# Gate matrices in a queue of their own, with two stages, their one-hots multiplied on GpSimd

## The chip, the cores and the metric

The kernel runs on one core of a Trainium2 chip. Its five engines are named as the profile names them: PE (TensorE, matmuls; PEld is its loading of weights), DVE (VectorE), ACT (ScalarE), POOL (GpSimd) and SP (SyncE, which here only issues DMAs). The metric is the device time of one execution in microseconds (us); less is better.

## The reference

One layer of a hybrid encoder for 1024 tokens of width 1024. Its first half is a token mixer (a convolution and an RWKV-7 recurrence side by side, then one output projection), its second a retrieval over 128 x 128 experts with one neuron each. Cut to what the change touches:

```python
s1 = einsum('bshd,hnd->bshn', q[..., :half], peer_k1)      # 8 heads, 128 keys each
s2 = einsum('bshd,hnd->bshn', q[..., half:], peer_k2)
v1, i1 = top_k(s1, 16); v2, i2 = top_k(s2, 16)
sc, ci = top_k((v1[..., :, None] + v2[..., None, :]).reshape(..., 256), 16)
experts = take(i1, ci // 16) * 128 + take(i2, ci % 16)     # 8 heads x 16 = 128 experts a token
gates = softmax(sc)
z = einsum('td,tkd->tk', h, peer_u[experts])
y = einsum('tk,tkd->td', gelu(z) * gates, peer_v[experts])
x = layer_norm(ALPHA * x + gate2 * y, ln2_g, ln2_b)
```

## The kernel before, in words

Tokens stand in eight tiles of 128. For the last three (GT = 5, 6, 7) the experts' rows are gathered from memory one by one. For the first five (DT) all 16384 experts are computed densely, and every activation is multiplied by a gate that is zero where the token did not choose the expert. These gates, 16384 for each token, are the gate matrices, and `gate_matrix` (line 921) makes them for one tile: the 128 choices of a token lie on partitions; a one-hot `oa` of the first index (line 940) and a one-hot `ob` of the second, multiplied by the gate (lines 943 to 956), are the operands of one 128x128x128 matmul for each token (line 958). Four tokens are one step: their matmuls fill one PSUM bank (`mgate`), ACT copies it into a stage of 32 tokens (line 959), and after eight steps the stage, 16 KB on each partition, is written to G_d in memory (line 961, a DMA that ACT issues). A tile has 32 steps and four stages. There is one stage buffer. Of each four steps one (POOL_OB) makes `ob` on DVE for all four tokens (line 944) and multiplies it on POOL (line 946); in the others DVE makes two of the one-hots with the gate in one instruction each (line 952), and ACT the other two with a square and a rectifier (lines 955 and 956).

The program is written as Python generators that are stepped by turns. First comes `inproj(0)`, then a loop over 16 chunks of 64 tokens (line 970) that carries the recurrence's state: `solve` prepares a chunk and `pass_state` carries the state through it (line 672 is its first step on DVE). Inside both stand calls of `fill` (line 565), which steps two lists: `side`, the long projections (`inproj(1)`, then one `post` for each 256 tokens: output projection, norms, queries at line 818, scores and their best 16 at line 835), and on every fourth fill (SLOW) `slow`, the small work: `conv` (both halves), `choose` for each tile (line 846, with products on POOL in line 902) and the gate matrices. `post` appends `choose` and the gate matrix of each of its tiles at line 842. The last post, for tiles 6 and 7, is appended behind the loop, where side steps and slow steps alternate (line 1008); the choices of its tiles run last of all (line 1022). Then come the dense experts (lines 1156 and 1190), in 32 groups, with the gathers of tiles 5, 6 and 7 between them (lines 1078 to 1093). They load the gates of a group from G_d (line 1133).

What is written gives each instruction its rank. The planner (`schedule_with_timeline_sim=True`) then puts each engine's instructions in an order: it simulates the engines and takes, of those whose inputs and buffers are there, the one with the first rank. On the chip each engine runs its list in order.

Memory is handed out by pools. `pgp` has NPAGE pages of 2 KB on a partition, in which nearly all temporary tiles lie; `ws` holds raw and split weight tiles (line 156: a raw tile is loaded once, split into two parts, and the parts are kept in memory for later posts); `fe` holds what only the input projections need. `fe` is closed at chunk 8, and `gb`, the gate matrices' pool, is opened in its place (line 977). Raw weights are last loaded by the first post.

Of the kernel before, what the change touches and what calls it, by code (L numbers as in the profile page):

```python
# [22 lines left out]
D = 1024  # L23
# [26 lines left out]

PSG, PSD = 3, 3
SLOW = 4
NTMP = 28
WRAW = 2
WSPLIT = 3
RUN = 4
STEPS = 4, 3
RATES = 1.0, 2.0
NPAGE = 35
TSLOW = 2  # L60
NCP = 12
CBUF = 4
GB = 3
DVE_OB = 2
POOL_OB = 1,
ABUF = 6
VBUF = 4

# [11 lines left out]
def layer_kernel(ctx, tc, x, cols, c_row, cond_w, w_in, w2a2, g2, w_out, ln_rows, wq, keys, peer_u, peer_ut, peer_v, peer_vt, out):  # L80
# [72 lines left out]
        return pgp.tile([128, max(w, 512)], dt, tag="pg", name=name)[:, :w]  # L153

    def load_raw(src):
        raw = ws.tile([128, KD, 128], F32, name="wraw", bufs=WRAW)
        ld(raw, src)
        return raw

# [80 lines left out]
    A.activation(sc, silc, AF.Sigmoid)  # L240
    V.tensor_mul(silc, sc, silc)

    def cond_some(js, pool=ws):

        for j in js:
            w = pool.tile([128, D], F32, tag="wraw", name="cw", bufs=WRAW if pool is ws else CBUF)
            ld(w, cond_w[j])
            V.scalar_tensor_tensor(w, w, 1.0, silc, op0=OP.mult, op1=OP.mult, accum_out=mod[:, j:j + 1])  # L248
        cs = slice(js[0], js[-1] + 1, js[1] - js[0])
        V.tensor_add(mod[:, cs], mod[:, cs], col("cond_b")[:, cs])  # L250
# [314 lines left out]
    def fill():  # L565

        credit[0] += rate[0]
        fills[0] += 1
        if credit[0] >= RUN:
            credit[0] -= RUN  # L570
            for _ in range(RUN):
                step(side)
        if fills[0] % SLOW == 0:
            slow_step(1)

    def pairs(n, fn):

# [168 lines left out]
    def post(t0, vpage):  # L746
# [93 lines left out]
                    yield  # L840
        for t in range(nt):
            (slow if vpage is page else tail).append(choose(tile0 + t, val[t], idx[t], vpage))
            if not fetch[t]:
                (slow if gb else gates).append(gate_matrix(tile0 + t))

    def choose(tt, val, idx, vpage):

        for _ in range(1):
            sh3 = [128, NH, TOPK]
            quad = lambda nm, dt=F32: vpage(nm, dt).rearrange("p (q h r) -> p q h r", q=4, h=NH)  # L850
            qf, qg, qu = quad("tkf"), quad("tkg"), quad("tku", U32)
            fp, m1, m2, m3 = (qf[:, i] for i in range(4))
            top, shf, fo = qg[:, 0], qg[:, 1], (qg[:, 2], qg[:, 3])
            pos = qu[:, 0]
            shi, qi_, ri_ = (qu[:, i].bitcast(I32) for i in (1, 2, 3))
            for hh in range(2):
                hs = slice(4 * hh, 4 * hh + 4)
                cand = vpage("cand")[:, :4 * NCAND].rearrange("p (h c) -> p h c", h=4)
                o = 0
                for i, m, w in REGIONS:  # L860
                    V.tensor_add(cand[:, :, o:o + m * w].rearrange("p h (a b) -> p h a b", b=w),
                                 val[:, hs, 0, i:i + m][:, :, :, None].to_broadcast([128, 4, m, w]),
                                 val[:, hs, 1, 0:w][:, :, None, :].to_broadcast([128, 4, m, w]))
                    o += m * w
                for h in range(4 * hh, 4 * hh + 4):
                    ch = cand[:, h - 4 * hh, :]
                    V.max(top[:, h, 0:8], ch)
                    V.max_index(pos[:, h, 0:8], top[:, h, 0:8], ch)
                    V.match_replace(ch, top[:, h, 0:8], ch, -3.0e38)
                    V.max(top[:, h, 8:16], ch)  # L870
                    V.max_index(pos[:, h, 8:16], top[:, h, 8:16], ch)
                    yield

            A.activation(fp, pos, AF.Copy)
            V.tensor_scalar(m1, fp, 32.0, None, op0=OP.is_ge)
            V.tensor_scalar(m2, fp, 48.0, None, op0=OP.is_ge)
            V.tensor_scalar(m3, fp, 64.0, None, op0=OP.is_ge)
            V.tensor_add(shf, m1, m2)
            V.scalar_tensor_tensor(shf, m3, 2.0, shf, op0=OP.mult, op1=OP.add)
            V.tensor_scalar(shi, shf, -1.0, 4.0, op0=OP.mult, op1=OP.add)  # L880
            V.tensor_tensor(qi_, pos.bitcast(I32), shi, op=OP.logical_shift_right)
            V.tensor_tensor(ri_, qi_, shi, op=OP.logical_shift_left)

            V.scalar_tensor_tensor(m1, m2, 3.0, m1, op0=OP.mult, op1=OP.add)
            V.scalar_tensor_tensor(m1, m3, 24.0, m1, op0=OP.mult, op1=OP.add)
            pb = lambda nm: vpage(nm, BF, 1024)
            qb = pb("tkb").rearrange("p (q h r) -> p q h r", q=8, h=NH)
            isel, jsel = qb[:, 0], qb[:, 1]
            V.scalar_tensor_tensor(isel, m1, -2.0, qi_, op0=OP.mult, op1=OP.add)
            V.tensor_sub(jsel, fp, ri_)  # L890
            for half, sel in ((0, isel), (1, jsel)):
                ib = qb[:, 2 + half]
                A.activation(ib, idx[:, :, half, :], AF.Copy)
                for hh in range(2):
                    hs = slice(4 * hh, 4 * hh + 4)
                    oh = pb("oh").rearrange("p (h q r) -> p h q r", h=4, q=TOPK)
                    sh4 = [128, 4, TOPK, TOPK]
                    V.tensor_tensor(oh, iota_q[:, None].to_broadcast(sh4), sel[:, hs, None, :].to_broadcast(sh4),
                                    op=OP.is_equal)
                    yield  # L900
                    E = G if vpage is page else V
                    E.tensor_mul(oh, oh, ib[:, hs, :, None].to_broadcast(sh4))
                    yield
                    for w in (8, 4, 2):
                        E.tensor_add(oh[:, :, 0:w], oh[:, :, 0:w], oh[:, :, w:2 * w])
                        yield
                    E.tensor_add(fo[half][:, hs], oh[:, :, 0], oh[:, :, 1])
                ld(sel_d[tt][half], fo[half].rearrange("p h r -> p (h r)"))
            mx = small.tile([128, NH], F32, name="mx")
            V.tensor_copy(mx, top[:, :, 0])  # L910
            V.tensor_sub(top, top, mx[:, :, None].to_broadcast([128, NH, TOPK]))
            A.activation(top, top, AF.Exp)
            sm = small.tile([128, NH], F32, name="sm")
            V.tensor_reduce(sm, top, axis=AX.X, op=OP.add)
            V.reciprocal(sm, sm)
            V.tensor_mul(top, top, sm[:, :, None].to_broadcast([128, NH, TOPK]))
            ld(sel_d[tt][2], top.rearrange("p h r -> p (h r)"))
            yield


    def gate_matrix(tt):
# [11 lines left out]
        neg = three("selneg")  # L933
        A.activation(neg, pt, AF.Copy, scale=-1.0)
        for r0 in range(0, 128, TB):
            stage = gb[0].tile([128, 128, TB], F32, name="stage", bufs=1)
            for q in range(0, TB, 4):
                ts = slice(r0 + q, r0 + q + 4)
                oa, ob = quad_("oa"), quad_("ob")
                V.tensor_tensor(oa, iota[:, None, :].to_broadcast([128, 4, 128]),  # L940
                                i1[:, ts, None].to_broadcast([128, 4, 128]), op=OP.is_equal)
                pt = mgate().rearrange("p (t e) -> p t e", t=4)
                if q // 4 % 4 in POOL_OB:
                    V.tensor_tensor(ob, iota[:, None, :].to_broadcast([128, 4, 128]),
                                    i2[:, ts, None].to_broadcast([128, 4, 128]), op=OP.is_equal)
                    G.tensor_mul(ob, ob, gt[:, ts, None].to_broadcast([128, 4, 128]))
                else:
                    for t in range(4):
                        c = slice(r0 + q + t, r0 + q + t + 1)
                        o = ob[:, t, :]  # L950
                        if t < DVE_OB:
                            V.tensor_scalar(o, iota, i2[:, c], gt[:, c], op0=OP.is_equal, op1=OP.mult)  # L952
                        else:

                            A.activation(o, iota, AF.Square, bias=neg[:, 1, c])
                            A.activation(o, o, AF.Relu, bias=gt[:, c], scale=neg[:, 2, c])
                for t in range(4):
                    T.matmul(pt[:, t, :], ob[:, t, :], oa[:, t, :], start=True, stop=True)  # L958
                A.activation(stage[:, :, q:q + 4], pt.rearrange("p t e -> p e t"), AF.Copy)  # L959
# [6 lines left out]
    side[:] = [first]  # L966
    rate[0] = RATES[0]
    drain(solve(0))
    flight = [[solve(1)]]
    for c in range(16):  # L970
        if c == 5:
            while side and side[0] is first:
                step(side)
        if c == 8:
            while conv_left:
                slow_step(1)
            fet.close()
            gb.append(fex.enter_context(tc.tile_pool(name="gb", bufs=1)))
            slow.extend(gates)
        if c < 14:  # L980
            flight.append([solve(c + 2)])
        for _ in pass_state(c):
# [8 lines left out]
        if c % 4 == 3 and c < 15:  # L991
            while late:
                step(late)
            side.append(post(64 * (c - 3), page))
            rate[0] = RATES[1]
    while late:
        step(late)
# [7 lines left out]
        return cp.tile([128, max(w, 512)], dt, tag="pg", name=name)[:, :w]  # L1005

    side.append(post(S - PB, cpage))
    while side or slow:
        step(side)
        fills[0] += 1  # L1010
        if fills[0] % TSLOW == 0 or not side:
            slow_step(1)

    h2h, h2l = ([dp.tile([128, ND], F32R, name=f"h2{w}{k}") for k in range(KD)] for w in "hl")
    for k in range(KD):
# [237 lines left out]
```

## Time and profile before

| | |
|---|---|
| median of 3 runs | 3366.39 us (3362.37 to 3373.07) |
| the profiled execution | 3369.74 us, span 3367.7 us |
| PE busy | 3039.8 us, 90% |
| DVE busy | 2523.1 us, 75% |
| POOL busy | 1734.8 us, 52% |
| ACT busy | 1246.3 us, 37% |
| granted TensorE clock, mean | 0.936 of full speed |

The page gives the busy time of each engine as a share of the span, a strip of the span in 40 slices, the chain of work that ended last, and the costliest groups of instructions. Shares over the whole span hide that the kernel has stages: the front end with the recurrence up to some 1540 us, the dense experts from there to the end. So the rows that are shown further down are taken stretch by stretch. A row of a group ends with the idle time of the engine just before its instructions and with what ended that idle time. Times in chains and windows are counted from the start of the span.

### The profile page before, as it was taken

The page shows a single profiled execution, that of the slowest core. Times are in us where ns is not written, and L with a number is a line of the kernel's source. Part 1 is how long each engine was busy: PE and PEld are TensorE (multiplying, and loading weights), DVE is VectorE, ACT ScalarE, POOL GpSimd, SP SyncE. Part 2 cuts the span into 40 slices and gives each one's busy share as a digit, 9 for nine tenths or more (in the row PEclk, how much of TensorE's full clock was granted, in tenths as well). Part 3 has the DMA queues.
Part 4 walks back from the last instruction along what each step waited for, and adds up shares of the span by engine and source line. Part 5 has one row for each costly group of instructions (what it writes and reads, how often), then busy time and mean ns, then how long its engine had stood idle before and what let it go on. Part 6 is the DMA issues. An engine that isn't in the chain of part 4 may idle for free.

```text
span 3367.7 us, 54601 instructions
## 1 busy us (share of the span) xinstructions
PE 3039.8 (90%) x20400; PEld 2652.4 (79%) x20400; DVE 2523.1 (75%) x5590; ACT 1246.3 (37%) x2479; POOL 1734.8 (52%) x1328
## 2 busy tenths in 40 slices
PE   6969999999888665676999999999999999999996
PEld 5735766678777665675899999999999989998985
DVE  5398567657676697779777778777787877777788
ACT  5552543443545435654322222322222232222222
POOL 2400112234122154313877777787777768777772
PEclk9979999799889777787999999999999999999998
DMA  8875564467556757465999999898999989999994
GB/s 307 292 258 170 163 178 163 155 236 269 168 194 206 250 173 230 141 213 174 360 345 330 348 333 342 323 361 324 356 330 346 327 327 347 349 337 342 332 345 163
DMA packets 398393, 918.09 MB, mean 273 GB/s; under 512 B 77184, under 2 KB 210480, under 8 KB 376112
## 3 DMA queue, kind: packets, MB, share of 16 engines
q1 hardware_dynamic: 205296, 469.96, 39.8%
q0 software_dynamic: 110592, 402.70, 32.4%
q10 hardware_dynamic: 82240, 41.94, 4.4%
q8 instruction: 160, 2.62, 0.3%
q14 instruction: 105, 0.86, 0.1%
HBM read 786.55 MB, written 127.95 MB: 272 GB/s over the span
## 4 chain that ended last, share of the span: by engine, by line
PE 71%; DVE 14%; DMA 8%; ACT 3%; issue 2%; POOL 1%; SPq 0%; DVEq 0%; POOLq 0%; ACTq 0%
PE mg L1156 25%; PE md L1190 25%; PE mm L182 11%; DMA G_d<-stage 5%; PE mgate L958 3%; DVE cacc L458 2%; DVE cw L248 1%; PE bank L635 1%; DVE oa L940 1%; DVE ob L952 1%; PE bank L655 1%; DMA cw<-cond_w 1%; PE mm L828 1%; PE mm L466 1%; PE bank L604 1%
## 5 line engine op out<-in xcount | busy, mean ns | idle before, releaser
L1156 PE MATMUL mg<-h2h,uhi 128*128 128x320 f32 x2048 | 634.0, 310 | 0.0
L1156 PE MATMUL mg<-h2l,uhi 128*128 128x320 f32 x2048 | 633.8, 309 | 0.0
L1156 PE MATMUL mg<-h2h,ulo 128*128 128x320 f32 x2048 | 633.5, 309 | 0.0
L1190 PE MATMUL md<-vhi,ah 128*128 128x512 f32 x1280 | 492.7, 391 | 23.0 <-ACT vhi L1119 16.1
L1190 PE MATMUL md<-vhi,al 128*128 128x512 f32 x1280 | 498.2, 390 | 0.0
L1190 PE MATMUL md<-vlo,ah 128*128 128x512 f32 x1280 | 497.0, 390 | 0.0
L1093 DVE SCALAR_TENSOR_TENSOR gy<-grow,gz,gy 128x1024 f32<-128x1024 f32 x381 | 488.6, 1282 | 6.4 <-DMA grow<-peer_v,eid 2.7
L1086 DVE SCALAR_TENSOR_TENSOR grow<-grow,gh 128x1024 f32<-128x1024 f32 x384 | 458.9, 1213 | 34.8 <-DMA grow<-peer_u,eid 30.9
L1078 POOL DMA_INDIRECT grow<-peer_v,eid x384 | 361.0, 940 | 163.4 <-DVE gy L1093 85.0
L1078 POOL DMA_INDIRECT grow<-peer_u,eid x384 | 361.4, 941 | 159.6 <-issue 70.8
L1156 PEld LDWEIGHTS mg<-h2h,uhi 128*128 128x128 f32 x2048 | 385.8, 188 | 6.0
L1156 PEld LDWEIGHTS mg<-h2l,uhi 128*128 128x128 f32 x2048 | 385.8, 188 | 5.1
L1156 PEld LDWEIGHTS mg<-h2h,ulo 128*128 128x128 f32 x2048 | 385.6, 188 | 3.9
L1119 ACT ACTIVATE vhi<-vraw 128x1024 fp32r<-128x1024 f32 x128 | 135.6, 1062 | 635.4 <-PE md L1190 434.8
L1195 DVE TENSOR_TENSOR yacc<-md,yacc 128x512 f32<-128x512 f32 x310 | 210.6, 688 | 186.5 <-PE md L1190 180.7
L1121 POOL TENSOR_TENSOR vlo<-vraw,vhi 128x1024 fp32r<-128x1024 f32 x128 | 306.3, 2414 | 68.7 <-ACT vhi L1119 62.7
L958 PE MATMUL mgate<-oa,ob 128*128 128x128 f32 x1280 | 213.3, 321 | 141.2 <-ACT stage L959 97.3
L1121 POOL TENSOR_TENSOR ulo<-uraw,uhi 128x1024 fp32r<-128x1024 f32 x128 | 310.9, 2429 | 50.0 <-ACT uhi L1119 43.6
L958 PEld LDWEIGHTS mgate<-oa,ob 128*128 128x128 f32 x1280 | 190.8, 228 | 154.3 <-ACT stage L959 92.2
L1190 PEld LDWEIGHTS md<-vhi,ah 128*128 128x128 f32 x1280 | 240.7, 188 | 70.7 <-ACT vhi L1119 16.4
L1190 PEld LDWEIGHTS md<-vlo,ah 128*128 128x128 f32 x1280 | 240.3, 188 | 48.5
L1190 PEld LDWEIGHTS md<-vhi,al 128*128 128x128 f32 x1280 | 240.3, 188 | 44.0
(347 smaller groups left out, 5837.7 us busy)
## 6 DMA issues: line engine op xcount, KB each, us to landing
uraw<-peer_ut SPq DMA_DIRECT2D x128, 512.0 KB
vraw<-peer_vt SPq DMA_DIRECT2D x128, 512.0 KB
wsplit<-split_wq SPq DMA_DIRECT2D x48, 1024.0 KB
G_d<-stage ACTq DMA_DIRECT2D x20, 2048.0 KB
gmat<-G_d SPq DMA_DIRECT2D x32, 1280.0 KB
cw<-cond_w SPq DMA_DIRECT2D x48, 512.0 KB
wsplit<-split_w_out SPq DMA_DIRECT2D x24, 1024.0 KB
split_w_in<-wsplit SPq DMA_DIRECT2D x22, 1024.0 KB
```

The costliest lines, as they stand in the source:

```text
L182: T.matmul(pt, l[:, k, :], r[k], start=i == 0, stop=i == 3 * KD - 1)
L248: V.scalar_tensor_tensor(w, w, 1.0, silc, op0=OP.mult, op1=OP.mult, accum_out=mod[:, j:j + 1])
L458: V.scalar_tensor_tensor(a, win(i), wk(i), a, op0=OP.mult, op1=OP.add)
L958: T.matmul(pt[:, t, :], ob[:, t, :], oa[:, t, :], start=True, stop=True)
L1078: G.indirect_dma_start(out=r, out_offset=None, in_=peer_u if k < 128 else peer_v, in_offset=bass.IndirectOffsetOnAxis(ap=eid[:, k % 128:k ...
L1086: V.scalar_tensor_tensor(r, r, 1.0, ht, op0=OP.mult, op1=OP.mult, accum_out=z[:, i:i + 1])
L1093: V.scalar_tensor_tensor(y, r, z[:, i - 128:i - 127], y, op0=OP.mult, op1=OP.add)
L1119: A.activation(hi, raw, AF.Copy)
L1121: G.tensor_sub(lo, raw, hi.bitcast(F32))
L1156: T.matmul(p, l[:, k, :], r[k][:, bs], start=i == 0, stop=i == 3 * KD - 1)
L1190: T.matmul(p, l[:, ts], r[:, e % 2, :], start=e == 0 and q == 0, stop=e == 3 and q == 2)
L1195: V.tensor_add(ya, p, ya)
```

## The change

`gates` becomes a queue of its own. `choose` appends the gate matrix of its tile when its selection has been stored. `fill` steps that queue on every twelfth fill (GSTEP) once `gb` is open, and the loop behind the chunks on every twelfth step (TGATE), or on each when `side` is empty. There are two stage buffers. In every step DVE compares three one-hots of `ob` in one instruction and POOL multiplies them by the gates; ACT makes the fourth. The raw weight tiles lie in `fe`, not in `ws`; `fe` is closed at chunk 9, after the first post has been stepped to its end; and `pgp` has 31 pages.

```diff
+GSTEP = 12
-NPAGE = 35
+NPAGE = 31
+TGATE = 12
-DVE_OB = 2
-POOL_OB = 1,
...
     def load_raw(src):
-        raw = ws.tile([128, KD, 128], F32, name="wraw", bufs=WRAW)
+        raw = fe.tile([128, KD, 128], F32, name="wraw", bufs=WRAW)
...
         if fills[0] % SLOW == 0:
             slow_step(1)
+        if gb and fills[0] % GSTEP == 0:
+            step(gates)
...
             (slow if vpage is page else tail).append(choose(tile0 + t, val[t], idx[t], vpage))
-            if not fetch[t]:
-                (slow if gb else gates).append(gate_matrix(tile0 + t))
...
             ld(sel_d[tt][2], top.rearrange("p h r -> p (h r)"))
+            if tt in DT:
+                gates.append(gate_matrix(tt))
...
-            stage = gb[0].tile([128, 128, TB], F32, name="stage", bufs=1)
+            stage = gb[0].tile([128, 128, TB], F32, name="stage", bufs=2)
...
-                if q // 4 % 4 in POOL_OB:
-                    V.tensor_tensor(ob, iota..., i2[:, ts, None]..., op=OP.is_equal)
-                    G.tensor_mul(ob, ob, gt[:, ts, None]...)
-                else:
-                    for t in range(4):
-                        if t < DVE_OB:
-                            V.tensor_scalar(o, iota, i2[:, c], gt[:, c], op0=OP.is_equal, op1=OP.mult)
-                        else:
-                            A.activation(o, iota, AF.Square, bias=neg[:, 1, c])
-                            A.activation(o, o, AF.Relu, bias=gt[:, c], scale=neg[:, 2, c])
+                V.tensor_tensor(ob[:, :3], iota..., i2[:, ts.start:ts.start + 3, None]..., op=OP.is_equal)
+                G.tensor_mul(ob[:, :3], ob[:, :3], gt[:, ts.start:ts.start + 3, None]...)
+                c, o = slice(ts.start + 3, ts.start + 4), ob[:, 3, :]
+                A.activation(o, iota, AF.Square, bias=neg[:, 1, c])
+                A.activation(o, o, AF.Relu, bias=gt[:, c], scale=neg[:, 2, c])
...
-        if c == 8:
+        if c == 9:
             while conv_left:
                 slow_step(1)
+            while side and side[0] is firsts[0]:
+                step(side)
             fet.close()
             gb.append(fex.enter_context(tc.tile_pool(name="gb", bufs=1)))
-            slow.extend(gates)
...
-    while side or slow:
+    while side or slow or gates:
         step(side)
         fills[0] += 1
         if fills[0] % TSLOW == 0 or not side:
             slow_step(1)
+        if fills[0] % TGATE == 0 or not side:
+            step(gates)
```

## Rows read from the trace of the kernel before

**Rows 1.** Busy us (and instructions) of each engine by stretch
```profile
core 0: us, PE busy (x) PEld busy (x) DVE busy (x) ACT busy (x) POOL busy (x), PEclk, DMA share, GB/s
310.00:785.00 475.00, 455.87 (x4463) 343.31 (x4465) 303.07 (x735) 198.22 (x403) 105.42 (x63) 0.92 0.56 178
785.00:1085.00 300.00, 260.25 (x2907) 235.55 (x2907) 218.00 (x847) 143.83 (x350) 78.37 (x73) 0.89 0.62 208
1085.00:1592.00 507.00, 331.83 (x2296) 315.86 (x2295) 409.91 (x1533) 258.81 (x639) 157.29 (x134) 0.80 0.58 193
1185.00:1285.00 100.00, 59.80 (x404) 56.67 (x404) 93.71 (x379) 32.20 (x85) 57.75 (x53) 0.78 0.55 191
1600.00:3200.00 1600.00, 1599.07 (x8996) 1460.25 (x8995) 1244.46 (x1874) 448.15 (x718) 1236.86 (x952) 1.00 0.92 340
```

**Rows 2.** Chain of waits, 1080 to 1610 us: shares; then start, us, what
```profile
by line: DMA G_d<-stage 32.6%; PE mgate L958 12.0%; PE mm L182 5.8%; ACT stage L959 3.6%; DVE oh L898 3.1%; DVE ob L952 2.8%; DVE oa L940 2.7%; issue 2.6%; ACT ob L956 2.1%; ACT ob L955 1.7%; DVE vi L839 1.6%; DVE s L837 1.6%; DVE vi L836 1
...
1539.45 9.67 DMA G_d<-stage
1549.19 6.26 DMA gmat<-G_d
...
1578.68 4.54 DVE oh L902 x4
...
1597.69 1.03 ACT gh L1071
...
1601.93 0.59 PE mg L1156 x4
```

**Rows 3.** Tile view of the stage: ns min/median/max, first and last start; idle
```profile
L959 ACT ACTIVATE stage<-mgate x160: 574/597/646, 846.7 to 1538.8; 128x512 f32<-128x512 f32 x160
...
  DMA G_d<-stage: 103.4, 17
```

**Rows 4.** The page's costliest groups: the gate matmuls
```profile
L958 PE MATMUL mgate<-oa,ob 128*128 128x128 f32 x1280 | 213.3, 321 | 141.2 <-ACT stage L959 97.3
```

**Rows 5.** Waits, 1225 to 1540 us: us in total, times, longest
```profile
ACT stage L959 <- DMA G_d<-stage: 70.9, 11, 11.8
DVE oa L940 <- PE mgate L958: 45.0, 18, 9.4
```

**Rows 6.** Groups on DVE, 785 to 1592 us: busy us, mean ns, idle before
```profile
L940 DVE TENSOR_TENSOR oa<-iota,selt 128x512 f32<-128x512 f32 x160 | 124.4, 778 | 104.5 <-PE mgate L958 97.9 <-ACT selt L931 6.0
L952 DVE TENSOR_SCALAR ob<-iota,selt 128x128 f32<-128x128 f32 x240 | 96.4, 442 | 0.0
...
L944 DVE TENSOR_TENSOR ob<-iota,selt 128x512 f32<-128x512 f32 x40 | 28.3, 708 | 0.0
```

**Rows 7.** Lines 952, 940, 835 by themselves: ns min/median/max
```profile
L952 DVE TENSOR_SCALAR ob<-iota,selt x240: 327/341/2376, 841.7 to 1534.1; 128x128 f32<-128x128 f32 x120
...
L940 DVE TENSOR_TENSOR oa<-iota,selt x160: 626/684/2393, 841.1 to 1533.2; 128x512 f32<-128x512 f32 x160
...
L835 DVE MAX8 vi<-s x128: 265/275/296, 720.6 to 1521.6; 128x8 f32<-128x128 f32 x128
```

**Rows 8.** Groups on ACT, 785 to 1592 us
```profile
L956 ACT ACTIVATE ob<-ob,selt,selneg 128x128 f32<-128x128 f32 x240 | 105.7, 488 | 3.6 <-DMA h2l<-h2t_d 3.6
...
L955 ACT ACTIVATE ob<-iota,selneg 128x128 f32<-128x128 f32 x240 | 82.4, 396 | 9.5 <-PE mgate L958 9.4
```

**Rows 9.** Groups on POOL, 785 to 1592 us
```profile
L946 POOL TENSOR_TENSOR ob<-ob,selt 128x512 f32<-128x512 f32 x40 | 45.0, 1126 | 396.4 <-DVE ob L944 245.0 <-DVE tkg L870 30.9 <-DMA h2t_d<-h2lo 23.6
```

**Rows 10.** Line 959 by stretch (one copy for each gate step)
```profile
785.00:1085.00 300.00, 25.71 (x44) 0.89 0.62 208
1085.00:1592.00 507.00, 67.17 (x117) 0.80 0.58 193
```

**Rows 11.** Lines 672 and 182, 310 to 785 us: first and last start
```profile
L672 DVE TENSOR_TENSOR Q<-Q,bank x9: 375/406/422, 379.0 to 768.0; 128x256 f32<-128x256 f32 x9
...
L182 PE MATMUL mm<-h2hi,wsplit x256: 277/283/682, 676.6 to 777.4; 128*128 128x256 f32 x128
```

More of the change, by code (lines that the diff above doesn't have):

```diff
@@ L241, in layer_kernel, with cond_some @@
     V.tensor_mul(silc, sc, silc)
-    def cond_some(js, pool=ws):
+    def cond_some(js, pool=fe):
         for j in js:
-            w = pool.tile([128, D], F32, tag="wraw", name="cw", bufs=WRAW if pool is ws else CBUF)
+            w = pool.tile([128, D], F32, tag="wraw", name="cw", bufs=WRAW if pool is fe else CBUF)
             ld(w, cond_w[j])
@@ L942, in gate_matrix @@
                 pt = mgate().rearrange("p (t e) -> p t e", t=4)
-                if q // 4 % 4 in POOL_OB:
-                    V.tensor_tensor(ob, iota[:, None, :].to_broadcast([128, 4, 128]),
-                                    i2[:, ts, None].to_broadcast([128, 4, 128]), op=OP.is_equal)
-                    G.tensor_mul(ob, ob, gt[:, ts, None].to_broadcast([128, 4, 128]))
-                else:
-                    for t in range(4):
-                        c = slice(r0 + q + t, r0 + q + t + 1)
-                        o = ob[:, t, :]
-                        if t < DVE_OB:
-                            V.tensor_scalar(o, iota, i2[:, c], gt[:, c], op0=OP.is_equal, op1=OP.mult)
-                        else:
-                            A.activation(o, iota, AF.Square, bias=neg[:, 1, c])
-                            A.activation(o, o, AF.Relu, bias=gt[:, c], scale=neg[:, 2, c])
+                V.tensor_tensor(ob[:, :3], iota[:, None, :].to_broadcast([128, 3, 128]),
+                                i2[:, ts.start:ts.start + 3, None].to_broadcast([128, 3, 128]), op=OP.is_equal)
+                G.tensor_mul(ob[:, :3], ob[:, :3], gt[:, ts.start:ts.start + 3, None].to_broadcast([128, 3, 128]))
+                c, o = slice(ts.start + 3, ts.start + 4), ob[:, 3, :]
+                A.activation(o, iota, AF.Square, bias=neg[:, 1, c])
+                A.activation(o, o, AF.Relu, bias=gt[:, c], scale=neg[:, 2, c])
                 for t in range(4):
@@ L968, in layer_kernel @@
     drain(solve(0))
-    flight = [[solve(1)]]
+    flight, firsts = [[solve(1)]], []
     for c in range(16):
@@ L994, in layer_kernel @@
             side.append(post(64 * (c - 3), page))
+            firsts.append(side[-1])
             rate[0] = RATES[1]
```

## The prediction

> **What bounds the kernel now.** I read the busy table by stage first [rows 1]. From 1600 us on PE is busy for 1599 of 1600 us: the expert stage is bound by PE, no line of it changes, and so it only moves with the moment at which it starts. Before 785 us PE is busy 456 of 475 us; there the change touches memory alone. In between, from 785 to 1592 us, just before the gather's first steps, no engine is full: PE 592 of 807 us (the two rows added), DVE 628, ACT 403, POOL 236. The chain of waits from 1080 us to the start of the experts says what sets the time there [rows 2]: 32.6% of some 530 us, about 173 us, is the write of the stage to G_d, far more than any engine's line. At its end stand the last such write (1539.45, 9.67 us), the load of the same data (1549.19), then DVE alone with the choices of the last two tiles (1578.68) and the gather's first ACT copy (1597.69). The tile view of the stage says why [rows 3]: there is one stage, so ACT's first copy into it waits for the DMA of the one before, 17 times of the 20, 103.4 us in all; the gate matmuls lack a PSUM bank meanwhile (97.3 us of idle PE [rows 4]). ACT and PE work in order, so all that is queued behind those two waits too. From 1225 to 1540 us the waits say it again [rows 5]: 70.9 us of ACT on the DMA, 45.0 us of DVE on gate matmuls.
>
> **The change part by part.** The sum is made against the profiled execution, 3369.7 us (span 3367.7); the runs shown have a median of 3366.4, 3.3 us below it, which is within their spread.
>
> *Second stage.* It takes the 17 waits away. A stage is eight groups of four tokens; eight groups cost DVE alone 8 x 1.56 = 12.5 us (249.1 us of lines 940, 952 and 944 over 160 groups [rows 6]), so a write of 9.67 us is covered by the building of the next stage, and a longer one nearly. What is late next is DVE: of the 507 us from 1085 to 1592 it is busy 409.9, 81% [rows 1]. So the term is what that DVE work takes once it can run on.
>
> *One-hots.* Removed on DVE: 240 short ones (96.4 us) and 40 of 512 elements (28.3) [rows 6]. Added: 160 of 384 elements, which the trace does not show; between the 341 ns of a 128-element one [rows 7] and the 708 ns of a 512-element one I take 3/4 of 708, 531 ns, the nearest row scaled: 85.0 us (54.6 to 113.3). DVE saves 124.7 - 85.0 = 39.7 us. ACT makes 160 one-hots in place of 240: 80 pairs of 488 + 396 ns fewer [rows 8], 71 us; ACT does not bound, so I count nothing, and if that is wrong it is a gain. POOL goes from 40 products of 1126 ns (45.0 us) to 160 of 3/4 of that, 845 ns, 135.1 us: 90.1 us more [rows 9].
>
> *What POOL costs DVE.* Short one-hots take 341 ns in the median and 2376 at most [rows 7]; mean 442 [rows 6], so 240 x 101 ns = 24 us were spent held. Line 940 has a median of 684 [rows 7] and a mean of 778: 160 x 94 = 15 us. That is 39 us on these two lines beside 236 us of POOL, 0.17 us for each us of POOL. On all lines it may be twice that: I take 0.35, so 90.1 x 0.35 = 32 us are added (0 to 90). DVE's net is then -39.7 + 32 = -8 us over 160 groups, and 117 of them stand after 1085 us [rows 10]: -6 us.
>
> By the Trainium skill (SBUF — State Buffer, § Who interferes with whom), a DVE instruction with two SBUF inputs and a GpSimd one that reads SBUF exclude each other for the whole instruction, and both compares here read two SBUF operands. Line 940 agrees in its extremes, 2393 ns against a median of 684 [rows 7]: it can sit out a whole POOL instruction. By that rule at its full price the DVE term would be +50 us and not -8; this is the second rival below.
>
> *Pace.* 409.9 - 6 = 404 us of DVE work from 1085 us to the gather's start. In the least disturbed 100 us of this stretch, 1185 to 1285, DVE is busy 93.7% [rows 1]; I take 92%. 404 / 0.92 = 439 us in place of 507: -68 us. Ends: as full as now, 81%, gives 499 (-8); all of it, 404 (-103).
>
> *State loop, 785 to 1085 us.* Gate steps come every twelfth fill and not every fourth, and only once their tile's choice is done. Each chunk's 64 fills of solving, 16 of passing and 4 of group norm set the pace, with PE at 260 of 300 us [rows 1]. Written order gives 31 gate steps there; the trace has 44 [rows 10]. 13 fewer are at most 13 x 1.56 = 20 us of DVE beside the passes. I count 0 (-20 to 0), since what is not done there is done later.
>
> *Memory.* 31 pages for 35. No row names a page wait. All that PE stands idle from 310 to 785 us is 19 us [rows 1]; the loss of four pages may cost nothing, or double that. I take 5 us (0 to 20). The raw tiles keep two buffers under one tag, 0. The gate memory opens one chunk later, after the first post's last load: that post's last projection is at 777.4 us, the last pass of the state before 785 us adds on DVE at 768.0 [rows 11], so what is forced there is about done: 0 (0 to 10).
>
> *Waits added.* The three loads of a selection now sit behind a finished choice, so SP is held less at them, and behind them on SP are only weight loads with three buffers. POOL's product waits for DVE's compare; behind it on POOL are the choices' products and the posts' additions. PE's gate matmul waits for the product, and behind it on PE stand the projections. If each of 160 products came 0.845 us late, that would be 135 us of PE; PE has 507 - 332 = 175 us idle after 1085 us [rows 1], so I take it as hidden there; where it is not, the pace is nearer to 81%.
>
> Sum: -68 + 0 + 5 = -63; 3369.7 - 63 = 3307 us.
>
> **Rivals.**
> 1. *DVE runs full.* Gate steps are ready early and of low rank, so the planner that orders each engine can drop them into every hole. -103, half of the 20 from the state loop and the 5 for pages: -108, about 3262 us. For it: 93.7% is already seen. Against it: PE, ACT and POOL are tied to each group, and queues work in order.
> 2. *POOL becomes the price.* All 90 us are taken from DVE: +50 over all groups, +37 after 1085, 447 / 0.92 = 486 us, -21 + 5: about 3354 us. For it: the 2376 ns, and that a gate product must queue on POOL behind the choices' longer ones. Against it: the maxima, a fair part of DVE's work, are never held (275 ns in the median, 296 at most [rows 7]).
> 3. *Gates are left over* (slower). A post is 612 steps (24 projections of 24 steps, 32 scores, four more), a fill takes two; by that count 856 steps remain after the state loop. With a gate step in twelve, 71 are done beside them, 31 before, and 58 of 160 stand alone behind the last post. If the planner does not pull them forward, DVE first has 410 - 117 x 1.56 - 52 (the last choices, from the last stage's write to 1592) = 176 us of other work and 71 x 1.31 = 93 of gates, 269 / 0.9 = 299 us; then 58 steps; then 52 us of choices. Alone, a step costs at least its DVE and POOL work, 0.684 + 0.531 + 0.845 = 2.06 us, and at most the whole round with 1.33 us of PE (213.3 / 160 [rows 4]) and 0.597 of ACT [rows 3], 3.99. Over (507 + 10 - 351) / 58 = 2.86 us it is slower, the 10 being what the state loop gains; at 3.4 it is +31: about 3401 us. For it: a low rate and a loop that drains the rest. Against it: by the same count the old gates' 160 steps are all written before half of the 856 steps, and they ran until 1539 us [rows 2], so the order moves with what is ready.
> 4. *No stage is hidden*, since memory only lets them share: the pools balance (four pages of 2 KB and two raw tiles of 4 KB make the 16 KB), so I give this nothing.
>
> **How the numbers follow.** Forecast (-25 to -95) 0.50, rival 1 0.14, rival 2 (-30 to +10) 0.19, rival 3 0.17. Told apart from no change is about 10 us, 0.3%. Faster: 0.50 + 0.14 + 0.11 of rival 2 = 0.75; same: 0.08, the rest of it; slower: 0.17. Below 3240 lies the corner of full DVE without any held time, some 0.05; above 3390 most of rival 3, some 0.1. So the range is 3240 to 3390; the forecast's own is 3275 to 3345.
>
> **What would show it.** Right: ACT's wait for the G_d write falls from 103 us below 20; that write leaves the chain but for the last one; DVE and POOL take its place; DVE busy over 90% between 1085 us and the first gather; the experts' second group of matmuls, now behind 1601.93 us [rows 2], comes near 1540. Second rival: means of line 940 near 1000 ns at an unchanged median. Third: a last stretch of gate steps with no projection beside them. Wrong altogether: a later last projection of the first post than 777 us (pages), or experts that no longer take the same time from their start to the end.

## The result and the profile after

The changed kernel takes 3321.86 us (median; 3307.2 to 3332.25), the kernel before in the same comparison 3365.66: a ratio of 0.9862 (95% interval 0.9832 to 0.9893). By the medians it is 44 us faster, by the ratio 1.4%. The forecast was 3307 us, 63 less than the profiled execution of before. The profiled execution of after took 3329.28 us, 40.5 less than that of before.

Busy time by stage, columns as in [rows 1]; the third line ends, as there, some 3 us before the first row of the gather:

```profile
310.00:785.00 475.00, 457.43 (x4318) 337.47 (x4318) 298.74 (x708) 196.92 (x400) 103.49 (x62) 0.91 0.54 172
785.00:1085.00 300.00, 272.41 (x2951) 243.58 (x2949) 248.50 (x920) 130.33 (x301) 121.43 (x121) 0.87 0.63 212
1085.00:1559.00 474.00, 354.34 (x2513) 332.41 (x2512) 421.98 (x1370) 239.18 (x549) 245.35 (x208) 0.86 0.64 214
...
1600.00:3200.00 1600.00, 1598.11 (x8983) 1458.76 (x8982) 1251.95 (x1867) 442.10 (x708) 1233.72 (x949) 1.00 0.93 339
```

From 1085 us to the gather there were 507 us and now there are 474. DVE is busy 422 of them, 89% (81% before), and POOL 245 (157 before). PE is busy 75% of that stretch, for 65%, and its granted clock is 0.86 of full speed, for 0.80: the 960 projection matmuls of line 182 there take 218 us and took 228, so some 10 us of PE time come with the higher clock. The experts are as full of PE as they were.

The tile view of the stage, against [rows 3], and below it the waits from 785 to 1545 us (total us, times, longest):

```profile
L955 ACT ACTIVATE stage<-mgate x160: 572/597/614, 862.2 to 1485.1; 128x512 f32<-128x512 f32 x160
L957 ACTq DMA_DIRECT2D G_d<-stage x20: 366/366/892, 900.2 to 1485.8; - x20
its engine sat idle before it (us, times) until:
  PE mgate L954: 125.4, 84
  DMA G_d<-stage: 0.9, 1
...
DMA to landing us min/median/max: 8.7/12.1/19.0
```

```profile
POOL ob L948 <- DVE ob L946: 129.9, 88, 11.5
ACT stage L955 <- PE mgate L954: 125.4, 84, 10.4
...
PE mgate L954 <- POOL ob L948: 76.6, 57, 8.6
DVE oa L942 <- PE mgate L954: 46.3, 22, 6.6
```

The 17 waits of 103.4 us for the write are one of 0.9. The last write is issued at 1485.8 us and was at 1539. PE now waits for the POOL product, 76.6 us; POOL waits for DVE's compare, and ACT for PE.

The groups on DVE and on POOL (busy us, mean ns, idle before), against [rows 6, 9], and their lines by themselves (ns min/median/max), against [rows 7]:

```profile
L942 DVE TENSOR_TENSOR oa<-iota,selt 128x512 f32<-128x512 f32 x160 | 133.3, 833 | 50.2 <-PE mgate L954 46.3 <-ACT selt L933 3.9
L946 DVE TENSOR_TENSOR ob<-iota,selt 128x384 f32<-128x384 f32 x160 | 130.3, 814 | 0.0
```

```profile
L948 POOL TENSOR_TENSOR ob<-ob,selt 128x384 f32<-128x384 f32 x160 | 167.1, 1047 | 251.3 <-DVE ob L946 129.9 <-DVE tkg L867 24.5 <-DVE tkg L870 22.2
```

```profile
L942 DVE TENSOR_TENSOR oa<-iota,selt x160: 631/681/2449, 856.6 to 1479.3; 128x512 f32<-128x512 f32 x160
L946 DVE TENSOR_TENSOR ob<-iota,selt x160: 499/551/2267, 857.8 to 1479.9; 128x384 f32<-128x384 f32 x160
L948 POOL TENSOR_TENSOR ob<-ob,selt x160: 817/827/5671, 858.9 to 1480.6; 128x384 f32<-128x384 f32 x160
L837 DVE MAX8 vi<-s x128: 248/275/296, 733.1 to 1484.4; 128x8 f32<-128x128 f32 x128
```

The chain of waits from 1500 us on (start, us, what), against the end of [rows 2]. This chain can be followed back to 1500.88 us and no further. From there on it holds the choices of the last tiles on DVE, and no write of the stage:

```profile
1508.74 4.53 DVE oh L902 x4
...
1522.50 5.29 DVE oh L905 x4
...
1544.87 3.41 DVE oh L902 x3
...
1553.49 1.41 PE md L1190 x5
1554.90 0.43 PE mg L1156 x3
```

Two rows give markers for what follows: the first matmul of the experts' second layer, which needs the G_d matrices, and the first row of the gather, which comes behind the choices of the last tiles, since its tiles take their memory. Before, then after (ns min/median/max, first and last start):

```profile
L1190 PE MATMUL md<-vhi,ah x1280: 387/389/797, 1562.1 to 3337.8; 128*128 128x512 f32 x183
...
L1078 POOL DMA_INDIRECT grow<-peer_u,eid x384: 932/937/1118, 1595.4 to 3020.3; - x192
```

```profile
L1190 PE MATMUL md<-vhi,ah x1280: 387/389/796, 1510.3 to 3294.4; 128*128 128x512 f32 x183
...
L1078 POOL DMA_INDIRECT grow<-peer_u,eid x384: 932/937/1118, 1562.2 to 2988.1; - x192
```

The gather starts 33.2 us earlier, and from there to the end of the span it is 1765.3 us (3327.5 - 1562.2) for 1772.3: the other 7 of the 40.2 us of span.

### The profile page after: what moved, and what is told of

The parts are those of the page before. It is cut to its first block, busy times and chain, and to the rows that moved or that the text cites. A ratio compares the mean times of both kernels' runs of the same rounds, so it can differ in the third digit from the quotient of the medians.

```text
span 3327.5 us, 54666 instructions
## 1 busy us (share of the span) xinstructions
PE 3055.9 (92%) x20400; PEld 2655.4 (80%) x20400; DVE 2561.4 (77%) x5470; ACT 1205.0 (36%) x2320; POOL 1862.2 (56%) x1448
## 3 DMA queue, kind: packets, MB, share of 16 engines
q0 software_dynamic: 110592, 402.70, 32.7%
## 4 chain that ended last, share of the span: by engine, by line
PE 48%; DVE 3%; DMA 2%; issue 1%; POOL 0%; ACT 0%; DVEq 0%; POOLq 0%
PE md L1190 24%; PE mg L1156 24%; DMA grow<-peer_u,eid 1%; DMA grow<-peer_v,eid 1%; DVE oh L902 0%; DVE grow L1086 0%; DVE oh L905 0%; POOL grow L1078 0%; DVE bnst L190 0%; DVE xres L1201 0%; DVE xres L1204 0%; DVE yacc L1195 0%; DVE mg L1160 0%; DVE gy L1093 0%; DVE xres L1205 0%
## 5 line engine op out<-in xcount | busy, mean ns | idle before, releaser
L948 POOL TENSOR_TENSOR ob<-ob,selt 128x384 f32<-128x384 f32 x160 | 167.1, 1047 | 251.3 <-DVE ob L946 129.9
L954 PE MATMUL mgate<-oa,ob 128*128 128x128 f32 x1280 | 210.1, 319 | 79.7 <-POOL ob L948 76.6
```

Of the source, the lines that this page charges most:

```text
L948: G.tensor_mul(ob[:, :3], ob[:, :3], gt[:, ts.start:ts.start + 3, None].to_broadcast([128, 3, 128]))
```

## The experiments

All ratios are against the kernel before, with a 95% interval. The table holds the markers of each profiled execution, in us: last start of the scores' first maxima (scores), issue of the last stage write (G_d), first start of the experts' second layer (2nd) and of the gather; then the span less 2nd and the span less gather.

```
kernel       ratio [interval]          scores  G_d    2nd    gather  span   -2nd   -gather
before       1                         1521.6  1539.4 1562.1 1595.4  3367.7 1805.6 1772.3
pages 31     0.9947 [0.9927, 0.9967]   1497.6  1513.8 1546.8 1573.1  3345.5 1798.7 1772.4
 one stage:
old, shared  0.9945 [0.9925, 0.9965]   1501.2  1534.9 1569.2 1589.9  3361.7 1792.5 1771.8
old, own     0.9931 [0.9911, 0.9951]   1472.2  1536.5 1568.1 1565.4  3350.9 1782.8 1785.5
POOL, shared 0.9912 [0.9890, 0.9933]   1465.8  1530.0 1561.5 1558.8  3346.1 1784.6 1787.3
POOL, own    1.0076 [1.0060, 1.0092]   1466.1  1572.4 1611.0 1582.9  3393.6 1782.6 1810.7
 two stages:
old, shared  0.9907 [0.9888, 0.9925]   1497.7  1472.7 1528.5 1581.3  3343.8 1815.3 1762.5
old, own     0.9864 [0.9841, 0.9886]   1481.4  1431.7 1511.9 1566.3  3328.3 1816.4 1762.0
POOL, shared 0.9947 [0.9929, 0.9966]   1500.8  1481.5 1532.1 1581.3  3342.9 1810.8 1761.6
after        0.9862 [0.9832, 0.9893]   1484.4  1485.8 1510.3 1562.2  3327.5 1817.2 1765.3
pages back   0.9848 [0.9825, 0.9870]   1469.1  1482.9 1504.7 1552.9  3320.0 1815.3 1767.1
two on ACT   0.9811 [0.9788, 0.9834]   1450.3  1466.1 1501.1 1536.3  3302.9 1801.8 1766.6
both of them 0.9770 [0.9747, 0.9793]   1451.4  1416.3 1480.3 1530.9  3292.1 1811.8 1761.2
no products  0.9756 [0.9738, 0.9775]   1431.4  1350.6 1462.4 1517.2  3280.5 1818.1 1763.3
```

"Old" and "POOL" are the one-hots of before and of after, "shared" and "own" the list from which gate steps are taken. All from "one stage" on lie on the memory of after. Each row of markers is of one execution, which can lie some 10 us from the median of its kernel (12 above it in "old, shared" with one stage, 8 below it in "POOL, shared" with two), so a marker difference of that size is no evidence by itself.

The last two columns fit two chains of which the later sets the end. In each of the eight kernels with two stages the end comes 1761 to 1767 us behind the gather, whatever the second layer does (1802 to 1818). In three kernels with one stage it comes 1783 to 1785 us behind the second layer, though their gather starts 12 to 37 us earlier than in the kernel before. In the kernel before and the two nearest to it neither figure is reached (1772 us, and 1793 to 1806). The ends of the traced chains, before and then after, fit this: before, PE's last matmuls stand there, after, the gather's last rows.

```profile
3312.34 15.46 PE md L1190 x68
3327.82 0.70 DVE yacc L1195
```

```profile
3265.56 13.41 DMA grow<-peer_v,eid
3279.06 1.30 DVE gy L1093
```

In all six kernels with one stage the traced chain ends behind PE's matmuls, in six of the eight with two behind the gather. "Pages back" and "two on ACT" are the exceptions: there it ends with PE, so the two chains lie close together.

**One stage again, all else as after.**

```diff
-            stage = gb[0].tile([128, 128, TB], F32, name="stage", bufs=2)
+            stage = gb[0].tile([128, 128, TB], F32, name="stage", bufs=1)
```

> The changed kernel with one stage buffer in place of two, all else as changed. Theory (the second stage pays, by taking ACT's waits for the G_d write away): those waits come back, near 100 us of idle ACT, and the time rises from about 3322 to 3365 us or more, since the new products on POOL still hold DVE. Rival (the products on POOL pay, by freeing ACT and the short compares on DVE): the time stays at 3320 to 3335 us, though ACT waits again. Rival (the queue of its own with its low rate pays): also 3320 to 3335 us.

1.0076: without its second buffer the change loses 0.8% where it gains 1.4%. The time is above the theory's 3365 us, and ACT's waits come back. The tile view of the stage and the line of the last maxima:

```profile
L957 ACTq DMA_DIRECT2D G_d<-stage x20: 366/366/425, 889.3 to 1572.4; - x20
its engine sat idle before it (us, times) until:
  PE mgate L954: 85.4, 70
  DMA G_d<-stage: 74.8, 13
```

```profile
L837 DVE MAX8 vi<-s x128: 266/275/296, 724.9 to 1466.1; 128x8 f32<-128x128 f32 x128
```

The last post is done 18 us earlier than in after, but the gate matrices run on for 106 us behind it. ACT's copies (x) count the gate steps in that stretch:

```profile
1466.00:1572.50 106.50, 22.71 (x40) 0.66 0.33 96
```

40 steps in 106.5 us, 2.66 us each, and PE meanwhile runs little but gate matmuls (start, us; idle before and its releaser):

```profile
1539.50 6.61 PE L954 MATMUL mgate<-oa,ob 128*128 128x128 f32 x32 [3.33 <-ACT stage L955]
...
1558.48 4.80 PE L954 MATMUL mgate<-oa,ob 128*128 128x128 f32 x24 [4.67 <-ACT stage L955]
1567.28 2.08 PE L954 MATMUL mgate<-oa,ob 128*128 128x128 f32 x8 [4.00 <-POOL ob L948]
```

That is the prediction's rival 3, gates left over. In this kernel the second stage is what keeps it away.

**The old one-hots, all else as after.** The diff is the one-hot part of the change, undone (`DVE_OB`, `POOL_OB` and the `if` over them are back).

```diff
-                V.tensor_tensor(ob[:, :3], iota..., i2[:, ts.start:ts.start + 3, None]..., op=OP.is_equal)
-                G.tensor_mul(ob[:, :3], ob[:, :3], gt[:, ts.start:ts.start + 3, None]...)
...
+                        if t < DVE_OB:
+                            V.tensor_scalar(o, iota, i2[:, c], gt[:, c], op0=OP.is_equal, op1=OP.mult)
```

> The changed kernel with the one-hots made as before (one step in four compared by DVE and multiplied on POOL, in the others two on DVE with the gate in one instruction and two on ACT), two stages, queue of its own. Theory: POOL's products cost DVE more than they save it, so the old one-hots are no slower: 3300 to 3330 us, with PE's waits for POOL's products (77 us in the changed kernel) gone and DVE's gate lines back near 249 us. Rival (the products pay): 3345 to 3365 us.

0.9864 against 0.9862, as the theory had it: no gain from the new one-hots can be seen in the full change. PE's wait for the POOL product falls from 77 to 25 us, and the gates are done 54 us sooner (1431.7), but the scores and the gather come within 4 us of where they did. On DVE the old one-hots do not come back to the 249 us that the theory named; they take 126.2 + 104.9 + 32.7 = 264 us, as long as the new ones in after:

```profile
L944 DVE TENSOR_TENSOR oa<-iota,selt 128x512 f32<-128x512 f32 x160 | 126.2, 788 | 46.5 <-PE mgate L963 45.1 <-ACT selt L935 1.1
L957 DVE TENSOR_SCALAR ob<-iota,selt 128x128 f32<-128x128 f32 x240 | 104.9, 471 | 0.0
L949 DVE TENSOR_TENSOR ob<-iota,selt 128x512 f32<-128x512 f32 x40 | 32.7, 818 | 0.0
```

**The shared list, all else as after.** `post` hands the gate matrix to `slow` again, behind the choice of its tile, and the steps on every twelfth fill and every twelfth step of the loop are gone.

```diff
-        if gb and fills[0] % GSTEP == 0:
-            step(gates)
...
+            if not fetch[t]:
+                (slow if gb else gates).append(gate_matrix(tile0 + t))
```

> The changed kernel with the gate matrices back in the list of the small work, behind the choices, at its rate; two stages and products on POOL stay. Theory (the planner puts gate steps where DVE has room whatever their written rate): 3310 to 3340 us, no clear difference from the changed kernel. Rival (the order pays): 3345 us or more, with the last G_d write later than 1510 us or the state's last pass later than 1090 us.

0.9947, 31 us above after: the theory (no difference) missed, and the rival had the time, but neither of its signs, for the last write is not late. The last scores start 16 us later than in after (1500.8) and the gather 19 us later, though the last write is at the same place (1481.5). By these markers the own queue with two stages does not serve the gates; it lets the last post through sooner. They account for 15 us of span, in an execution 8 us below its median; where the rest arises was not traced.

**Two stages alone**: shared list and old one-hots, both diffs above.

> Of the change only the two stages and the memory for them (31 pages, raw tiles in the front end's memory, that closed at chunk 9); one-hots and queue as before. Theory (the second stage alone pays): 3305 to 3335 us, as fast as the whole change. Rival (it takes all three parts): 3340 to 3370 us.

0.9907, 3340.73 us, just inside the rival's range: the second stage alone does not do what the whole change does. ACT's waits for the write are gone here too, and the last write comes 67 us earlier than before; but the scores end at 1497.7, and the gather follows them. The gain stops where the other chain begins.

```profile
L964 ACTq DMA_DIRECT2D G_d<-stage x20: 366/367/417, 898.4 to 1472.7; - x20
its engine sat idle before it (us, times) until:
  PE mgate L961: 110.4, 67
  DMA G_d<-stage: 2.7, 2
```

**The queue alone**: one stage, old one-hots.

> The changed kernel with one stage and the old one-hots: of the three parts the queue alone. Theory (the second stage pays whatever the queue and the one-hots are): 3370 to 3400 us, 40 us or more above the same with two stages (3327). Rival (the large loss with one stage, 73 us, came of POOL's products standing in each step): 3330 to 3355 us.

0.9931, in the rival's range. The scores are early (1472.2), ACT still waits 17 times, 99.8 us, and by the table the second layer is last.

```profile
  DMA G_d<-stage: 99.8, 17
```

**The products alone**: one stage, shared list.

> The changed kernel with one stage and the shared list: of the three parts POOL's products alone. Theory (the products do not pay by themselves): 3370 to 3400 us, no faster than the memory alone. Rival (with one stage they pay, by shortening the building of a stage, which then stands before each write): 3340 to 3360 us.

0.9912, again in the rival's range and not the theory's, with early scores too (1465.8) and the second layer last.

**None of the three**: one stage, shared list, old one-hots, on the memory of after.

> The kernel before with the change's memory alone (31 pages, raw tiles in the front end's memory, closed at chunk 9): one stage, old one-hots, one list. 31 pages alone gave 3348 us, 18 us below before, against what both theories had, so the memory also reorders the plan. Theory (the second stage pays on its own): 3350 to 3385 us, 15 us or more above the same kernel with two stages (3341), with ACT's waits for the G_d write at 60 to 105 us. Rival (the plan's order and not the stage gave those 30 us): 3335 to 3345 us.

0.9945, 18 us below the kernel before, by memory alone, and by the ratios 13 us above the same with two stages (0.9907), a little less than the theory's 15.

**31 pages in the kernel before.**

```diff
-NPAGE = 35
+NPAGE = 31
```

> The kernel before with 31 pages for 35 and nothing else. Theory (the 12 to 14 us by which the changed kernel is behind at 530 us come from the four pages): the store of mod_d, at 519 us before, comes at 528 to 535 us, and the time is 3372 to 3385 us. Rival (they come from the raw tiles in the other pool or from chance of the order): 519 +- 3 us and no difference.

0.9947. Four pages fewer make the kernel before faster, against every expectation. The store of the modulation behind the second input projection (mod_d) is 4 us later (issued at 528.3 us for 524.3; the expectations put these stores some 5 us earlier than the traces); the last scores come 24 us earlier and ACT waits 70 us for the write and not 103. The number of pages changes what the planner sees, so the order of all the work around the gates is another one. Which piece of that order pays was not found out; it stays open.

**Four pages given back in after**, from memory that the front end has free at that time.

```diff
-        lo = [page("hlo", F32R) for _ in range(KD)]
+        lo = [fe.tile([128, 512], F32R, name=f"hlo{k}") if h == 1 and k < 4 else page("hlo", F32R) for k in range(KD)]
```

> The changed kernel with four of the second half's sixteen input tiles (hlo 0 to 3) in the front end's memory, which has room for them; so the second projection has 35 pages' worth again. Theory (pages cost 12 to 14 us there, and the whole front end is a chain that passes them on): mod_d's store is back at 517 to 522 us, and the time falls by 8 to 15 us, to about 3310. Rival (the later stretches have slack that swallows it): the store is earlier, and the time stays within 4 us of the changed kernel.

0.9848. mod_d is stored at 523.5 us (537.8 in after), so the missing pages do cost 14 us there; at the end 4 us are left (3317.95 us), inside the intervals, as the rival had it. The chain of this kernel, otherwise that of after, can be followed through the whole stretch (1080 to 1610 us, shares), and no write of the stage stands in it:

```profile
by line: PE mm L182 12.5%; PE mgate L954 9.6%; DVE ob L946 8.2%; DVE oa L942 8.0%; issue 7.5%; POOL ob L948 4.7%; PE md L1190 4.3%; DMA wsplit<-split_wq 2.8%; DVE vi L838 2.4%; DVE s L839 2.3%; DMA grow<-peer_u,eid 2.2%; PE mm L830 2.2%; DV
```

**Two of four one-hots on ACT**, two on DVE and POOL.

```diff
-                V.tensor_tensor(ob[:, :3], iota..., i2[:, ts.start:ts.start + 3, None]..., op=OP.is_equal)
+                V.tensor_tensor(ob[:, :2], iota..., i2[:, ts.start:ts.start + 2, None]..., op=OP.is_equal)
...
-                c, o = slice(ts.start + 3, ts.start + 4), ob[:, 3, :]
+                for t in (2, 3):
+                    c, o = slice(ts.start + t, ts.start + t + 1), ob[:, t, :]
```

> The changed kernel with two of each four gated one-hots on ACT and two compared on DVE and multiplied on POOL, for one and three. Theory (DVE and POOL together bound the stretch after 785 us: one of them is busy for 746 of 807 us, while ACT is busy for 383): DVE's compares fall by some 20 us and POOL's products by 45, and the time falls by 10 to 30 us, to 3290 to 3312. Rival (the last post and the choices behind it bound, not the gates): 3315 to 3330 us. Rival (ACT's order, with the stage copies on it, becomes the wait): slower than 3330.

0.9811 (3307.44 us), 14 us below after, in the theory's range; but the gain is no larger than what a new order alone brought. The compare falls from 130.3 to 95.5 us, the product from 167.1 to 122.3, and ACT, busy 461 of 748 us, has the room:

```profile
L942 DVE TENSOR_TENSOR oa<-iota,selt 128x512 f32<-128x512 f32 x160 | 130.3, 814 | 67.0 <-PE mgate L954 64.2 <-ACT selt L933 2.6
L946 DVE TENSOR_TENSOR ob<-iota,selt 128x256 f32<-128x256 f32 x160 | 95.5, 597 | 0.0
```

**No products.** Three of four one-hots are not multiplied by their gates, so the experts' sum is another.

```diff
-                G.tensor_mul(ob[:, :3], ob[:, :3], gt[:, ts.start:ts.start + 3, None]...)
```

> The changed kernel without POOL's products: three of four one-hots are not multiplied by their gates, so the experts' sum is another; all else is as changed. It measures what the 160 products cost. By the prediction's term (0.35 us of DVE for each of the 135 us of POOL, so 47 us, at a pace of 0.92 some 50): 3270 to 3280 us. By the measured hold on the gates' two lines (66 us, of which 39 were there before): 27 us, 3290 to 3300. Rival (the last post and the choices behind it bound): 3310 to 3325.

0.9756 (3285.65 us): without the 160 products the kernel is 36 us faster, between the two ranges. DVE's two gate lines without them:

```profile
L942 DVE TENSOR_TENSOR oa<-iota,selt 128x512 f32<-128x512 f32 x160 | 123.8, 774 | 32.1 <-PE mgate L953 31.8
L946 DVE TENSOR_TENSOR ob<-iota,selt 128x384 f32<-128x384 f32 x160 | 107.3, 671 | 0.0
```

These lines hold (833 - 774 + 814 - 671) x 160 = 32 us less of DVE. With DVE 87% busy from 785 us to the gather (670.5 of 774), 32 / 0.87 is 37, about the 36. That fits a price paid on DVE and does not prove it: PE's 76.6 us of waits for the product are gone as well, and the order is a new one.

**Both of these on after**: the pages given back and two one-hots on ACT.

> The changed kernel with two of four one-hots on ACT (which gave 3307 us) and four tiles of the second projection in the front end's memory (which gave 3318 and an earlier store of mod_d, 519 for 533 us). If both gains pass on to the end: 3295 to 3303 us. If the earlier store is swallowed by the stretch behind it: 3303 to 3310 us. By the spread that a new plan alone gives (18 us from four pages) 3285 to 3325 is possible.

0.9770 (3293.86 us), 2.3% below the kernel before and faster than after too, 1 us below the expected 3295 to 3303.

The eight kernels of all three switches say how far to trust a single effect. The second stage is worth 0.4% with the old one-hots on the shared list (0.9945 to 0.9907), 0.7% with them on the own queue (0.9931 to 0.9864), 2.1% with the products on the own queue (1.0076 to 0.9862), and costs 0.35% with the products on the shared list (0.9912 to 0.9947). Since a mere re-planning moved the time by 0.5%, no effect of that size is put down to a mechanism here. The 2.1% is: there the G_d chain is last without the second stage and not with it. In the order memory, second stage, queue, one-hots the change's gain is made up of some 18, 13, 14 and 1 us (0.9945, 0.9907, 0.9864, 0.9862); in another order the parts are others.

## Why the prediction was right, and where its sizes were not

*The second stage* did what was said: 103.4 us of waits became 0.9, no write stands in the chain as far as it can be followed, and DVE was fuller next. The term was too large: -68 us were given to the stretch from 1085 us to the gather, and it fell by 33. The prediction had 404 us of DVE work at 92% in 439; measured are 422 at 89% in 474. The work accounts for 20 of the missing 35 (18 / 0.92), the pace for the rest. By the runs the second stage by itself is worth 13 us with the old one-hots on the shared list and 23 on the own queue. What the prediction did not see is that the G_d chain, once short, leaves a second chain that was nearly as late: the stages alone, against one stage on the same memory and list, brought the write 62 us forward (1534.9 to 1472.7) and the gather 9 (1589.9 to 1581.3).

*The one-hots.* This step failed in its sum. The net on DVE was to be -8 us; lines 942 and 946 take 263.6 us (133.3 + 130.3) where the three lines of before took 249.1 [rows 6], so +14.5. The price of the new compare was nearly right (551 ns in the median, 531 taken), and so was the hold: 160 x (833 - 681) + 160 x (814 - 551) = 66 us on the two lines, 27 more than the 39 of before; 32 had been added. Wrong was the saving of 39.7. It set busy time with its hold in it (96.4 us for the short compares) against the new compare at its free price. Free against free, the gates went from 160 x 0.684 + 240 x 0.341 + 40 x 0.684 (the median of line 944) = 219 us to 160 x (0.681 + 0.551) = 197: 22 saved, and 27 of hold eat them. The remaining 10 is that the old short compares overlapped: their mean times their count is 106 us, their busy time 96.4. Not all of the 14.5 is the exchange, though. With that one switch changed and the rest kept, the gate lines go from 264 to 264 us (two stages, own queue), 265 to 275 (two, shared), 252 to 261 (one, shared) and 254 to 256 (one, own): 0 to 10 us more, and never 8 less.

By the Trainium skill (SBUF — State Buffer, § Who interferes with whom) a DVE instruction with two SBUF inputs and a GpSimd one that reads SBUF exclude each other for the whole instruction. The maxima of 2449 and 2267 ns agree: one compare can sit out a whole product. The prediction's full price of +50 us was another claim, that DVE loses all the time that POOL gains, and it was too high: without the 167 us of products the compares took 32 us less, and the products were held in their turn, 160 x (1047 - 827) = 35 us.

*POOL's products* have the median that was estimated (827 ns, 845 taken), but a mean of 1047 and a maximum of 5671: 167 us, not 135.

*State loop and queue.* 0 was taken, by fewer gate steps. ACT's copies number 37 there, not 44 (31 by the written order), but DVE is busier, not less, 248.5 us for 218.0, and the last pass of the state starts some 11 us later (1079 us for 1068). The queue has no other term in the sum, since what is not done early is done later. That step failed: with two stages the own queue is worth 14 us with the old one-hots (0.9907 to 0.9864) and 29 with the products (0.9947 to 0.9862); only the second is above what a new order alone brought. By the markers it works on the last post and the gather, not on the gates.

*Memory.* The local cost is 14 us at mod_d, within the 0 to 20 given, and 12 us at the last projection of the first post:

```profile
L182 PE MATMUL mm<-h2hi,wsplit x256: 277/283/682, 689.6 to 789.7; 128*128 128x256 f32 x128
```

It was at 777.4 [rows 11], and a later one was named as the sign of a wrong prediction; the sign came, and the kernel was faster all the same. At the end the sign of the term was wrong: the pages alone made the kernel before 18 us faster, by an order that nobody had predicted. If the effects add, some 18 of the 44 us came from a source that the prediction did not have, and the reasons that it did have brought nearer 26 than 63. That the total came so near to the forecast is in this part luck.

*Rivals.* DVE did not run full (89%). POOL became a price, but not the whole one: line 942 has a mean of 833 ns and not 1000. The gates were not left over: the last write is issued 1.4 us behind the start of the last scores. With one stage they are, at 2.66 us a step against the 2.06 to 3.99 given. No stage is hidden, the fourth, got no chance and did not come: the wait for the write is gone.

*Named in advance:* ACT's wait below 20 us, yes (0.9). The write out of the chain: yes from 1500.88 us on, and over the whole stretch in "pages back", where DVE, POOL and PE stand in its place. DVE over 90%, barely not (89%). Experts' second group of matmuls near 1540 us: the first piece of line 1156 behind the choices in the chain starts at 1555, for 1602. The same time for the experts from start to end, else a sign of being wrong: 7 us less by the gather, 12 more by the second layer, so they do not only move with their start.

## What to carry to other kernels

Before a wait is removed, find the chain that ends next behind it: here the span less the gather's first row was 1761 to 1767 us in every kernel with two stages, the span less the second layer's first matmul 1783 to 1785 in three with one, and in the kernels between the chains were too close for the markers to part them. Compare an old and a new instruction both free of contention, and add the contention afterwards. When a list scheduler orders the work, run the incidental part of a change alone (here four pages fewer), for it can bring as much as the part that was meant. Count what a queue delays, too, and not only what it serves.

## What the runs showed that was not expected

Both sides of the DVE and POOL contention can be read from medians and maxima: the compare takes 551 ns alone and up to 2267, the product 827 and up to 5671, while the maxima of line 837 stay at 248 to 296 throughout. Held compares are those with POOL work beside them: of the 160 of line 946, the 83 with no POOL instruction beside them take 566 ns at most, the 77 with one 1103 in the mean; of line 942, 53 take 698 at most and 107 take 910 in the mean. Held time on the gate lines per us of POOL from 785 us to the gather hardly moved with the load: 39 of 236 before (0.17), 66 of 367 after (0.18).
